# A first norm whose weights go on at the eviction, and norms and attention blocks moved into neighbouring stages of a two-layer trunk

## The chip, the cores and the metric

The kernel runs on one core of a Trainium2 chip. Its time is the device time of one execution, in microseconds (us); lower is better. Three runs of the kernel before gave 3104.6, 3106.2 and 3106.36 us, median 3106.2. Five engines work side by side, each through its own list of instructions: TensorE (PE in the profile, its weight loads PEld), VectorE (DVE), ScalarE (ACT), GpSimd (POOL) and SyncE (SP), which issues nearly all the DMAs.

## The reference

512 tokens of width 1024 pass two layers, in fp32. Layer 0 mixes by a convolution module and a gated linear attention; layer 1 by a forgetting attention (FoX, 16 heads of 64, causal, in query blocks of 128). Each layer ends with a PEER block: every token picks 128 of 16384 experts by product keys. Every mixing and every PEER block starts with an RMS norm, so there are four:

```
def rms_norm(x, g):
    y = x * rsqrt(mean(x * x, axis=-1, keepdims=True) + EPS)
    return y * g

h = rms_norm(x, ev_norm_mix);  x = x + even_mix(h, ...)      # norm 0, layer 0
h = rms_norm(x, ffn_norm[0]);  x = x + peer_ffn(h, ...)      # norm 1
h = rms_norm(x, od_norm_mix);  x = x + fox_mix(h, ...)       # norm 2, layer 1
h = rms_norm(x, ffn_norm[1]);  x = x + peer_ffn(h, ...)      # norm 3

# fox_mix, per head and query block i: softmax(q k^T * scale + c_q - c_k, causal) v, then o @ w_out
# peer_ffn: act = gelu(h @ u^T); out = (gate * act) @ v
```

## The kernel before

**Products.** fp32 operands are split in two parts, high and low (`split`, L51 and L52: ACT rounds the high part, DVE or POOL subtracts it to give the low one), and every product is three matmuls: high by high, low by high, high by low (`mm3`, L78, L79, L80). A weight tile is 128x1024: a DMA into `raw` (4 buffers), `whi` on ACT, `wlo` on DVE or POOL (3 buffers each).

**Tokens** lie in four blocks of 128 (`xb[0]` to `xb[3]`; block 0 stays in SBUF, the others are kept in DRAM during PEER). A norm (`rms_h`, `rms_body`) goes block by block. `scale(b)`: ACT squares the block and sums it (`sq`, L105), DVE makes the mean (`ss`, L106), POOL the power -0.5 (`rs`, L107), DVE multiplies the block by it and by the gains (`xs`, L108; the gains, `grow`, are one row broadcast to 128 partitions, a DMA of 512 KB, L86). `flip(b)`: PE transposes the block in eight 128x128 pieces, four into one PSUM bank (L115); ACT writes the high part `hhi` from the bank (L117), DVE the low part `hlo` (L118). The projections that follow contract over `hhi` and `hlo`.

**PSUM** has eight banks here: a pool `a` of six (scores, transposes and the accumulators of the projections) and a pool `b` of two.

**Stages.** Norm 0 and the layer-0 projections; the output projection of layer 0 (`out_proj`, two halves of the columns, c = 0 and 1, each four accumulators and weights in four slices; its additions to x are L200); norm 1; PEER of layer 0 (`peer`, `peer_body`): query projections (`q`, L928) interleaved with u tiles (`u_step`, accumulators `pu` over the 384 tokens of blocks 1 to 3, evicted by ACT through a gelu, L854), gathers of expert rows by DMA and, last, the sweeps over v tiles (`v_sweep`, L1033) into accumulators whose sums are added to x (L1062). Then norm 2, FoX, its output projection, norm 3 and the second PEER in the same way. In FoX one `unit()` is a score block of a head and a query block: scores (L640, L641) into one bank, row maximum on DVE (L643), exp on ACT (L646), reciprocal and scaling on DVE (L647, L648), transposes (L659) into another bank, a copy out (`PT`, L662 on ACT for four blocks, L664 on DVE for fewer), and the product with v (`po`, L672). Units are spread between the matmuls of the head projections; the last `8 + AHEAD + 1` come after the last projection and before `out_proj`.

**Order.** The program is written in Python and a scheduler orders each engine's instructions by simulated times; each engine then runs its list in that order, waiting at an instruction for what it reads. DMAs of one queue share semaphores in turn, so the ninth DMA issued waits for the first to land.

Of the kernel before, what the change touches and what calls it, by code (L numbers as in the profile page):

```python
# [45 lines left out]
class Trunk:  # L46
# [8 lines left out]
    def weight(self, src, shape=None, eng=None, after=None):  # L55

        nc = self.nc
        raw = self.ws.tile([P, D], F32, tag="raw", name="raw", bufs=4)
        self.last_raw = nc.sync.dma_start(raw, src)
        hi = self.ws.tile([P, D], F32R, tag="whi", name="whi", bufs=3)  # L60
        lo = self.ws.tile([P, D], F32R, tag="wlo", name="wlo", bufs=3)
# [26 lines left out]
    def rms_h(self, i, hT, h0=None, order=range(NB), after=None):  # L88


        with self.tc.tile_pool(name=f"rms{i}", bufs=1, reuse_waits="tile") as rp:
            self.rms_body(rp, i, hT, h0, order, after)
        if i + 1 < 4:
            self.load_gain(i + 1)

    def rms_body(self, rp, i, hT, h0, order, after):
        nc = self.nc
        xs = {}

        def scale(b):  # L100
            ss = self.np.tile([P, 1], F32, name="ss", bufs=NB)
            rs = self.np.tile([P, 1], F32, name="rs", bufs=NB)
            xs[b] = h0 if b == 0 and h0 is not None else rp.tile([P, D], F32, name="xs", bufs=2)
            sq = rp.tile([P, D], F32, name="sq")
            self.last_sq = nc.scalar.activation(sq, self.xb[b], AF.Square, accum_out=ss)  # L105
            nc.vector.tensor_scalar(ss, ss, 1.0 / D, EPS, op0=ALU.mult, op1=ALU.add)  # L106
            nc.gpsimd.tensor_tensor(rs, ss, self.mhalf, op=ALU.pow)  # L107
            nc.vector.scalar_tensor_tensor(xs[b], self.xb[b], rs, self.grow, op0=ALU.mult, op1=ALU.mult)  # L108

        def flip(b):  # L110
            for c in range(2):
                p = self.bank([P, 4, P])
                for k in range(4):
                    kk = (4 * c + k) * P
                    nc.tensor.transpose(p[:, k], xs[b][:, kk:kk + P], self.ident)  # L115
                hi, lo = [h[:, 4 * c:4 * c + 4, b * P:(b + 1) * P] for h in hT]
                nc.scalar.activation(hi, p, AF.Copy)  # L117
                nc.vector.tensor_tensor(lo, p, hi.bitcast(F32), op=ALU.subtract)  # L118

        scale(order[0])  # L120
        for n, b in enumerate(order):
            if n + 1 < NB:
                scale(order[n + 1])
            flip(b)
            if after:
                after(b)
# [27 lines left out]
    def nat_parts(self, srcs, hT, lead=0, order=range(4), done=None, between=None, eng=None):  # L154
        acc = [self.bank() for _ in range(NB)]

        def load(kps):
            return [(kp, *self.weight(srcs[kp], (2, 512), eng)) for kp in kps]

        def sweep(ws, blocks):  # L160
            for kp, wh, wl in ws:
                for a in range(2):
                    k = 2 * kp + a
                    for b in blocks:
                        s = slice(b * P, (b + 1) * P)
                        self.mm3(acc[b], hT[0][k][:, s], hT[1][k][:, s], wh[:, a], wl[:, a],
                                 kp == order[0] and a == 0, kp == order[-1] and a == 1)

        first = load(order[:lead])

        def rest():
            end = 1 if done else 4
            for kp in order[lead:end]:
                sweep(load([kp]), range(NB))
                if between:
                    between()
            if done:
                ws = load(order[end:])
                for b in BLOCKS:
                    sweep(ws, [b])  # L180
                    done(b, acc[b])
# [13 lines left out]
    def out_proj(self, w, yT, order=range(4)):  # L195
# [6 lines left out]
        for b, acc in enumerate(self.proj_nat(w[0], yT, order=order)):  # L202
            add(0, b, acc)
        self.proj_nat(w[1], yT, order=order, done=lambda b, acc: add(1, b, acc))
# [24 lines left out]
    def mix_even(self):  # L229
        nc, tc, A = self.nc, self.tc, self.A  # L230
        hT = self.new_hT()
        with tc.tile_pool(name="m0c", bufs=1) as sc:
            self.rms_h(0, hT)
            self.mix_even_body(hT, sc)

# [944 lines left out]
```

## Time and profile before

| | |
|---|---|
| median of three runs | 3106.2 us |
| the profiled execution: time, span, granted clock | 3103.41 us, 3101.6 us, 0.996 |
| PE busy | 3058.7 us, 99% of the span |
| DVE, ACT, POOL busy | 2401.2 (77%), 1384.7 (45%), 1096.6 us (35%) |
| HBM traffic | 253 GB/s over the span |

Span and busy times are of one execution. Part 4 of the page, the chain of work that ended last, lies for 92% on PE. Times in the rows are counted from the start of the span; `[idle before <-releaser]` at a row's end says how long the engine stood idle before it and what it waited for. PEclk is the granted clock of TensorE as a share of 2.4 GHz.

### The profile page before, as it was taken

Reading aid. Unit: us, or ns where it says so; the run is one execution under the profiler, and the core shown is the slowest. Engines: PE = TensorE matmul, PEld = TensorE weight load, DVE = VectorE, ACT = ScalarE, POOL = GpSimd, SP = SyncE. Lnnn points to the kernel's source line nnn. Section 1 sums busy time; section 2 is a strip of 40 time slices with the busy share of each in tenths; the row PEclk is TensorE's granted clock in tenths of the full one; section 3 lists DMA queues with packets and bytes.
Section 4 is the critical chain, followed back from the end, with each engine's and each line's share of the span. In section 5 each row is a group of like instructions: output and inputs, shape, how many; then the busy total and the mean of one; then the engine's idle time right before and its main releaser. Section 6 shows DMA issues by size and latency. Waiting matters only on the chain.

```text
span 3101.6 us, 45719 instructions
## 1 busy us (share of the span) xinstructions
PE 3058.7 (99%) x15932; PEld 2684.7 (87%) x15932; DVE 2401.2 (77%) x4936; ACT 1384.7 (45%) x2224; POOL 1096.6 (35%) x800
## 2 busy tenths in 40 slices
PE   8999999999999999999999999999999999999999
PEld 6668999999999888888776679999999998888887
DVE  6764998888886888888645638898888867888886
ACT  4444334666664333333344523336666653333332
POOL 1220122976674222222100000227866752222220
PEclk9999999999999999999999999999999999999999
DMA  4113444999999899999421124448999998999996
GB/s 158 55 35 116 137 144 159 353 363 336 343 320 329 298 356 363 366 363 370 172 82 42 42 78 142 137 142 311 380 336 345 336 326 278 356 369 357 376 363 219
DMA packets 334201, 787.15 MB, mean 254 GB/s; under 512 B 26745, under 2 KB 181770, under 8 KB 327826
## 3 DMA queue, kind: packets, MB, share of 16 engines
q1 hardware_dynamic: 260242, 515.76, 47.5%
q0 software_dynamic: 73728, 268.47, 24.5%
q8 instruction: 125, 2.05, 0.3%
q14 instruction: 106, 0.87, 0.1%
HBM read 687.59 MB, written 96.47 MB: 253 GB/s over the span
## 4 chain that ended last, share of the span: by engine, by line
PE 92%; DVE 3%; issue 2%; DMA 1%; POOL 1%; ACT 1%; DVEq 0%; POOLq 0%; ACTq 0%
PE acc L1033 32%; PE pu L79 11%; PE pu L80 11%; PE pu L78 11%; PE bank L78 6%; PE bank L80 5%; PE bank L79 5%; PE bank L912 5%; PE pc L285 1%; PE po L672 1%; PE bank L640 1%; PE bank L936 1%; DMA gr<-in_uN_dram,ids 1%; DVE wlo L52 1%; PE bank L659 1%
## 5 line engine op out<-in xcount | busy, mean ns | idle before, releaser
L51 ACT ACTIVATE whi<-raw 128x1024 fp32r<-128x1024 f32 x604 | 639.8, 1060 | 1500.6 <-issue 584.8
L52 DVE TENSOR_TENSOR wlo<-raw,whi 128x1024 fp32r<-128x1024 f32 x565 | 692.4, 1226 | 339.1 <-ACT whi L51 309.7
L78 PE MATMUL pu<-hhi,whi 128*128 128x384 f32 x2048 | 699.1, 341 | 1.2 <-ACT hhi L117 1.2
L80 PE MATMUL pu<-hhi,wlo 128*128 128x384 f32 x2048 | 688.2, 336 | 2.6 <-DVE wlo L52 2.6
L79 PE MATMUL pu<-hlo,whi 128*128 128x384 f32 x2048 | 686.8, 335 | 0.0
L873 POOL DMA_INDIRECT gr<-in_vF_dram,ids x256 | 277.0, 1082 | 720.8 <-DVE x L875 696.2
L1033 PE MATMUL acc<-wlo,wh 128*128 128x512 f32 x1536 | 439.2, 389 | 0.0
L1033 PE MATMUL acc<-whi,wh 128*128 128x512 f32 x1536 | 439.1, 389 | 0.0
L862 POOL DMA_INDIRECT gr<-in_uN_dram,ids x256 | 349.2, 1364 | 252.4 <-DVE dots L864 157.3
L1033 PE MATMUL acc<-whi,wl 128*128 128x512 f32 x1536 | 436.8, 389 | 0.0
L78 PEld LDWEIGHTS pu<-hhi,whi 128*128 128x128 f32 x2048 | 386.2, 189 | 3.0 <-ACT hhi L117 1.7
L80 PEld LDWEIGHTS pu<-hhi,wlo 128*128 128x128 f32 x2048 | 385.6, 188 | 3.4 <-DVE wlo L52 3.2
L79 PEld LDWEIGHTS pu<-hlo,whi 128*128 128x128 f32 x2048 | 386.2, 189 | 1.7 <-DVE hlo L118 0.3
L1033 PEld LDWEIGHTS acc<-whi,wl 128*128 128x128 f32 x1536 | 288.4, 188 | 59.9
L1033 PEld LDWEIGHTS acc<-wlo,wh 128*128 128x128 f32 x1536 | 288.4, 188 | 59.7
L1033 PEld LDWEIGHTS acc<-whi,wh 128*128 128x128 f32 x1536 | 288.4, 188 | 59.5
L875 DVE SCALAR_TENSOR_TENSOR x<-gr,dots,x 128x1024 f32<-128x1024 f32 x256 | 327.2, 1278 | 0.0
L864 DVE CUSTOM_DVE_ANT_0 gr<-gr,h 128x1024 f32<-128x1024 f32 x256 | 308.6, 1225 | 20.9 <-DMA gr<-in_uN_dram,ids 20.7
L902 POOL TENSOR_SCALAR a<-cst,sT 128x128 f32<-128x128 f32 x192 | 316.3, 1648 | 15.2 <-PE bank L912 5.6
L52 POOL TENSOR_TENSOR wlo<-raw,whi 128x1024 fp32r<-128x1024 f32 x39 | 98.1, 2515 | 396.1 <-ACT whi L51 388.1
L899 DVE TENSOR_TENSOR a<-cst,sT 128x512 f32<-128x512 f32 x192 | 133.4, 695 | 126.2 <-PE bank L912 114.8
L78 PE MATMUL bank<-hhi,whi 128*128 128x512 f32 x512 | 211.5, 414 | 3.5 <-DVE hlo L118 2.7
(244 smaller groups left out, 4095.7 us busy)
## 6 DMA issues: line engine op xcount, KB each, us to landing
raw<-in_uT_dram SPq DMA_DIRECT2D x256, 512.0 KB
raw<-in_vF_dram SPq DMA_DIRECT2D x256, 512.0 KB
G<-big SPq DMA_DIRECT2D x48, 1024.0 KB
gc<-G SPq DMA_DIRECT2D x32, 1536.0 KB
aside<-xact SPq DMA_DIRECT2D x208, 192.0 KB
at<-aside SPq DMA_DIRECT2D x104, 384.0 KB
raw<-in_w_in_dram SPq DMA_DIRECT2D x32, 512.0 KB
raw<-in_wq_dram SPq DMA_DIRECT2D x32, 512.0 KB
```

Of the source, the lines that this page charges most:

```text
L51: first = self.nc.scalar.activation(hi, raw, AF.Copy)
L52: self.last_lo = (eng or self.nc.vector).tensor_tensor(lo, raw, hi.bitcast(F32), op=ALU.subtract)
L78: mm(out, lh, rh, start=first, stop=False)
L79: mm(out, lh, rl, start=False, stop=False)
L80: return mm(out, ll, rh, start=False, stop=last)
L862: nc.gpsimd.indirect_dma_start(out=r, out_offset=None, in_=uN, in_offset=bass.IndirectOffsetOnAxis(ap=ids[:, s:s + 1], axis=0))
L864: return lambda: nc.vector.tensor_tensor_reduce(r, r, h0, 1.0, 0.0, ALU.mult, ALU.add, accum_out=dots[:, s:s + 1])
L873: nc.gpsimd.indirect_dma_start(out=r, out_offset=None, in_=vF, in_offset=bass.IndirectOffsetOnAxis(ap=ids[:, s:s + 1], axis=0))
L875: return lambda: nc.vector.scalar_tensor_tensor(self.x0, r, dots[:, s:s + 1], self.x0, op0=ALU.mult, op1=ALU.add)
L902: (nc.vector if t else nc.gpsimd).tensor_scalar(a1[:, t], self.iota, e1[:, t:t + 1], gate[:, t:t + 1], op0=ALU.is_equal, op1=ALU.mult)
L912: nc.tensor.matmul(p[:, t], a2[:, t], a1[:, t], start=True, stop=True)
L1033: nc.tensor.matmul(acc[b][c], wt[:, s], vt[:, c], start=(n == 0 and wt is wh and vt is vh), stop=(n == NE1 - 1 and wt is wl))
```

## The change

**First norm.** `first_norm` replaces `rms_h(0)`. The gains come as a column `gc` (128x8, 4 KB), x of blocks 1 to 3 is loaded right behind it, and four weight tiles before the other constants; the broadcast row is not loaded for this norm. The blocks are scaled by their token factor alone (`tensor_scalar`); the transposes go by the column tile k, four blocks into one bank, and the gain is applied at the eviction, where it is one number per partition: `scale=gc` on ACT, a `scalar_tensor_tensor` on DVE.

**The other norms** are built by `norm`, which gives out `scale` and `flip`, so that callers place them. Squares are written into the `xs` buffer instead of one of their own. Norm 2 is begun in the tail of the first PEER (`odd_begin`): block 0 is scaled and flipped between the last v sweeps, and the first two weight slices of the v projection get a pool of their own. Norm 3 is begun in the second half of the output projection (`ends`): blocks 1, 2, 3 are finished one after the other, each added, kept and scaled, and their flips stand between the matmuls of block 0; `chain` keeps this order on PE. The first `u_step` of each PEER stands before the flip of block 0.

**Attention.** The last twelve calls of `unit()` are made in the first half of the output projection, four behind each of three weight slices (`between`).

```
-    def rms_h(self, i, hT, h0=None, order=range(NB), after=None):
...
+    def norm(self, i, blocks=3):
...
+        def scale(b, dst=None):
...
+            xs[b] = rp.tile([P, D], F32, name="xs", bufs=blocks) if dst is None else dst
+            self.last_sq = nc.scalar.activation(xs[b], self.xb[b], AF.Square, accum_out=ss)
...
+        def flip(b, hT, other=False):
             for c in range(2):
-                p = self.bank([P, 4, P])
+                p = self.ps.tile([P, 4, P], F32, tag="b", name="fl", bufs=2) if other else self.bank([P, 4, P])
...
+    def chain(self):
+        last = []
+        def run(f, *args):
+            if last:
+                with self.tc.issue_after(last.pop().ins):
+                    last.append(f(*args))
...
+    def out_proj(self, w, yT, order=range(4), i=None, hT=None, between=None, middle=None):
...
+        def ends(sweeps, acc):
+            run = self.chain()
+            def finish(b):
+                add(1, b, acc[b])
+                if b:
+                    nc.sync.dma_start(self.kept[b - 1], self.xb[b])
+                    scale(b)
+            for b in DB:
+                for f in sweeps:
+                    run(f, b)
+                finish(b)
+            for n, f in enumerate(sweeps):
+                if n == 0:
+                    run(flip, 1, hT)
+                    run(flip, 2, hT)
+                if n == 2:
+                    run(flip, 3, hT)
+                run(f, 0)
+            finish(0)
...
+    def first_norm(self, gc, hT):
...
+                nc.vector.tensor_scalar(xs[b], self.xb[b], rs, None, op0=ALU.mult)
+            for k in range(KD):
+                p = self.bank([P, NB, P])
+                for b in range(NB):
+                    nc.tensor.transpose(p[:, b], xs[b][:, k * P:(k + 1) * P], self.ident)
+                p = p.rearrange("p b t -> p (b t)")
+                nc.scalar.activation(hT[0][:, k], p, AF.Copy, scale=gc[:, k:k + 1])
+                nc.vector.scalar_tensor_tensor(hT[1][:, k], p, gc[:, k:k + 1], hT[0][:, k].bitcast(F32),
+                                               op0=ALU.mult, op1=ALU.subtract)
...
-            for _ in range(8 + AHEAD + 1):
-                unit()
-            self.out_proj(A["w_out1"], self.rows(oT))
+            self.hT = self.new_hT()
+            self.out_proj(A["w_out1"], self.rows(oT), i=3, hT=self.hT, between=lambda: [unit() for _ in range(4)],
+                          middle=lambda: pool.__exit__(None, None, None))
...
+            if L == 0:
...
+                scale, flip, close = self.norm(1, 2)
+                scale(1)
+                for b in DB:
+                    scale((b + 1) % NB, None if b < NB - 1 else h0)
+                    flip(b, hT)
...
-        nu = 0
+        run(lambda: u_step(0)[1])
+        nu = 1
+        last()
...
         for b in range(nd):
-            v_sweep(tail, b)
+            run(v_sweep, tail, b)
...
+            if L == 0:
+                scale(DB[b])
+                if b == 1:
+                    run(put, 0, hN, True)
+        if L == 0:
+            for b in DB:
+                run(put, b, hN, True)
+                run(start, b - 1)
+            run(start, NB - 1)
```

`last` flips block 0 (`run(flip, 0, hT)`) and closes the norm's pools; `put` is the `flip` of norm 2 and `start(b)` the first eight products of block b in the v projection. The scheduler's order changes at the start, between layer 0 and its PEER, between that PEER and FoX, and from the last attention blocks into the second PEER; elsewhere the lists are the same but for the order of the very last v sweeps.

PE's list at the start, before: transposes (L115) come block by block, and the first products (L78 to L80) behind those of the fourth block; `wgh` is a small weight of the gate.

```order
L115 MATMUL bank<-cst,xs 128x128 [waits DVE_49]
L115 MATMUL bank<-cst,xs 128x128 x3
L115 MATMUL bank<-cst,xs 128x128 [waits PE_49]
L115 MATMUL bank<-cst,xs 128x128 x3
L78 MATMUL bank<-hhi,whi 128x512 [waits DVE_49,Activation_49]
L78 MATMUL bank<-hhi,whi 128x512 [waits DVE_49,PE_49]
L78 MATMUL bank<-hhi,wgh 16x512 [waits DVE_49]
L78 MATMUL bank<-hhi,whi 128x512 [waits DVE_49,PE_49,Activation_49]
L79 MATMUL bank<-hlo,whi 128x512 [waits DVE_49]
```

And of the change, the last transposes (L322) and the first products (L87 to L89):

```order
L322 MATMUL bank<-cst,xs 128x128 [waits DVE_49]
L322 MATMUL bank<-cst,xs 128x128 x5
L322 MATMUL bank<-cst,xs 128x128 [waits DVE_49]
L322 MATMUL bank<-cst,xs 128x128 x3
L322 MATMUL bank<-cst,xs 128x128 [waits DVE_49]
L322 MATMUL bank<-cst,xs 128x128 x3
L87 MATMUL bank<-hhi,whi 128x512 [waits DVE_49]
L88 MATMUL bank<-hlo,whi 128x512
L89 MATMUL bank<-hhi,wlo 128x512 [waits Pool_49]
```

The transposes of each block come in a run of six, and those of the last two column tiles behind them; the products of one weight tile then follow each other, one column tile after the other.

ACT's list from the end of the output projection of layer 1 into the second PEER, before: `sq` are the squares, `whi` the high parts of weights, `hhi` those of the norm, `q` the query projections, `xact` the gelus.

```order
L105 ACTIVATE sq,ss<-x_72 128x1024 [waits DVE_49,Activation_49]
L51 ACTIVATE whi<-raw 128x1024 [waits DMAHW1_49,PE_49]
L51 ACTIVATE whi<-raw 128x1024 [waits DMAHW2_49,PE_49]
L51 ACTIVATE whi<-raw 128x1024 [waits DMAHW3_49,PE_49]
L117 ACTIVATE hhi<-bank 128x4x128 [waits PE_49] x8
L51 ACTIVATE whi<-raw 128x1024 [waits DMAHW4_49,DVE_49,PE_49]
L51 ACTIVATE whi<-raw 128x1024 [waits DMAHW2_49,PE_49]
L928 ACTIVATE q<-bank 128x512 [waits PE_49]
L51 ACTIVATE whi<-raw 128x1024 [waits DMAHW3_49,PE_49]
L928 ACTIVATE q<-bank 128x512 [waits PE_49]
L854 ACT_TABLE_LOAD
L854 ACTIVATE xact<-pu 128x384 [waits PE_49]
```

And of the change, where L109 are the squares, L122 `hhi`, L1050 `q` and L972 the gelu:

```order
L122 ACTIVATE hhi<-bank 128x4x128 [waits PE_49]
L109 ACTIVATE xs,ss<-x 128x1024 [waits DVE_49]
L122 ACTIVATE hhi<-bank 128x4x128 [waits PE_49] x3
L53 ACTIVATE whi<-raw 128x1024 [waits DMAHW1_49,PE_49]
L122 ACTIVATE hhi<-bank 128x4x128 [waits PE_49] x2
L109 ACTIVATE h_16452,ss<-x_72 128x1024 [waits DMAHW3_49,DMAHW2_49,DMAHW4_49,DVE_49,Activation_49]
L53 ACTIVATE whi<-raw 128x1024 [waits DMAHW2_49,Activation_49]
L53 ACTIVATE whi<-raw 128x1024 [waits DMAHW3_49,Activation_49]
L53 ACTIVATE whi<-raw 128x1024 [waits DMAHW4_49,PE_49,Activation_49]
L972 ACT_TABLE_LOAD
L972 ACTIVATE xact<-pu 128x384 [waits PE_49]
L122 ACTIVATE hhi<-bank 128x4x128 [waits PE_49] x2
```

The eight `hhi` stood together ahead of all gelus; now six stand among the squares and weights, and the two of block 0 stand behind the table load and the first gelu. PE's list between the last attention blocks, before, has the scores (L640, L641), the transposes (L659) and `po` (L672) by themselves; these rows are from the end of that stretch, ahead of the output projection (L78 to L80 with `ohi`):

```order
L659 MATMUL bank<-cst,pr 128x128 [waits DVE_49,Activation_49]
L659 MATMUL bank<-cst,pr 128x128 x2
L640 MATMUL bank<-ka_14268,qa_14266 128x384 [waits PE_49]
L641 LDWEIGHTS idb
L641 MATMUL bank<-nmask,idb 128x128
L659 MATMUL bank<-cst,pr 128x128 [waits DVE_49,Activation_49]
L659 MATMUL bank<-cst,pr 128x128 x3
L640 MATMUL bank<-ka_14268,qa_14266 128x512 [waits PE_49]
L641 LDWEIGHTS idb
L641 MATMUL bank<-nmask,idb 128x128
L659 MATMUL bank<-cst,pr 128x128 [waits DVE_49,Activation_49]
L672 MATMUL po<-PT,v 64x512 [waits Activation_49]
```

Of the change, in the first half of the output projection (L87 to L89), scores are L747 and L748, transposes L766, `po` L779:

```order
L747 MATMUL bank<-ka_14264,qa_14262 128x384 [waits DVE_49]
L748 LDWEIGHTS idb
L748 MATMUL bank<-nmask,idb 128x128
L766 MATMUL bank<-cst,pr 128x128 [waits Activation_49]
L766 MATMUL bank<-cst,pr 128x128 x3
L747 MATMUL bank<-ka_14264,qa_14262 128x512 [waits Activation_49]
L748 LDWEIGHTS idb
L748 MATMUL bank<-nmask,idb 128x128
L779 MATMUL po<-PT,v 64x512
L779 MATMUL po<-PT,v 64x384
L779 MATMUL po<-PT,v 64x256
L779 MATMUL po<-PT,v 64x128
```

The last blocks now stand among the output projection's matmuls. There four of the six banks of pool `a` hold accumulators, so that scores and transposes take turns in the other two, and a row that waits for Activation or DVE next to another bank's use waits for the copy out of it.

## Rows read from the trace of the kernel before

**Rows 1.** the page: busy time of the engines, share of the span and instructions

```profile
PE 3058.7 (99%) x15932; PEld 2684.7 (87%) x15932; DVE 2401.2 (77%) x4936; ACT 1384.7 (45%) x2224; POOL 1096.6 (35%) x800
```

**Rows 2.** five stretches: length, busy time (instructions) by engine, granted clock, DMA share, GB/s

```profile
0.00:30.00 30.00, 14.86 (x50) 11.16 (x51) 15.30 (x22) 14.46 (x27) 5.89 (x10) 0.89 0.74 253
272.00:282.00 10.00, 5.42 (x31) 3.85 (x30) 9.68 (x13) 7.77 (x13) 0.55 (x1) 0.83 0.41 116
1525.00:1545.00 20.00, 16.66 (x86) 13.61 (x85) 13.62 (x18) 9.10 (x15) 10.61 (x6) 1.00 0.31 105
1764.00:1788.00 24.00, 22.97 (x114) 13.97 (x114) 17.81 (x52) 12.05 (x32) 0.00 (x0) 1.00 0.07 23
1836.00:1855.00 19.00, 12.97 (x59) 11.63 (x60) 13.81 (x20) 8.38 (x14) 3.21 (x4) 0.73 0.25 83
```

**Rows 3.** timeline of PE at the start: start us, us, what, idle before

```profile
20.44 0.50 PE L78 MATMUL bank<-hhi,whi 128*128 128x512 f32 x1 [0.88 <-ACT hhi L117]
...
24.62 0.80 PE L79 MATMUL bank<-hlo,whi 128*128 128x512 f32 x1 [0.87 <-DVE hlo L118]
...
29.06 0.54 PE L80 MATMUL bank<-hhi,wlo 128*128 128x512 f32 x1
...
29.67 0.40 PE L79 MATMUL bank<-hlo,whi 128*128 128x512 f32 x1
29.91 0.39 PE L80 MATMUL bank<-hhi,wlo 128*128 128x512 f32 x1
```

**Rows 4.** the same view of ACT, DVE and SP at the start

```profile
4.42 1.06 ACT L105 ACTIVATE sq<-x 128x1024 f32<-128x1024 f32 x1 [2.42 <-DMA x<-in_x_dram]
...
9.06 1.29 DVE L108 SCALAR_TENSOR_TENSOR xs<-x,rs,grow 128x1024 f32<-128x1024 f32 x1 [3.30 <-DMA grow<-in_gains_dram]
...
10.30 1.06 ACT L105 ACTIVATE sq<-x 128x1024 f32<-128x1024 f32 x1 [4.12 <-DMA x<-in_x_dram]
...
11.52 3.33 SPq L59 DMA_DIRECT2D raw<-in_w_in_dram  x4
```

**Rows 5.** timeline between layer 0 and its PEER, DVE and PE

```profile
276.21 3.49 DVE L52 TENSOR_TENSOR wlo<-raw,whi 128x1024 fp32r<-128x1024 f32 x3
...
280.45 1.30 PE L78 MATMUL bank<-hhi,whi 128*128 128x512 f32 x2 [1.53 <-DVE hlo L118]
```

**Rows 6.** timeline of PE in norm 2

```profile
1538.93 1.06 PE L115 MATMUL bank<-cst,xs 128*128 128x128 f32 x8 [1.83 <-DVE xs L108]
```

**Rows 7.** groups in the last attention blocks: busy us, mean ns, idle before

```profile
L643 DVE TENSOR_REDUCE nm<-bank 128x1 f32<-128x512 f32 x3 | 2.1, 685 | 0.6 <-PE bank L641 0.6
...
L646 ACT ACTIVATE pr<-bank,nm 128x512 f32<-128x512 f32 x3 | 2.1, 688 | 1.4 <-DVE nm L643 1.4
...
L648 DVE TENSOR_SCALAR pr<-pr,den 128x512 f32<-128x512 f32 x3 | 1.4, 483 | 0.1
...
L662 ACT ACTIVATE PT<-bank 128x512 f32<-128x512 f32 x4 | 2.4, 598 | 3.8 <-PE bank L659 3.8
```

**Rows 8.** timeline from the output projection of layer 1 into the second PEER

```profile
1835.19 0.40 PE L80 MATMUL bank<-whi,olo 128*128 128x512 f32 x1
...
1836.41 1.06 ACT L105 ACTIVATE sq<-x 128x1024 f32<-128x1024 f32 x1 [3.05 <-DVE ss L106]
...
1837.04 1.29 DVE L108 SCALAR_TENSOR_TENSOR xs<-x,rs,grow 128x1024 f32<-128x1024 f32 x1 [0.66 <-POOL rs L107]
...
1837.47 2.93 ACT L51 ACTIVATE whi<-raw 128x1024 fp32r<-128x1024 f32 x3
...
1838.39 4.66 PE L115 MATMUL bank<-cst,xs 128*128 128x128 f32 x24 [2.79 <-DVE ss L106]
...
1847.09 1.94 PE L115 MATMUL bank<-cst,h 128*128 128x128 f32 x8 [3.29 <-DVE hlo L118]
...
1854.57 0.33 PE L79 MATMUL pu<-hlo,whi 128*128 128x384 f32 x1
```

**Rows 9.** all groups of the span: the gelu's table loads

```profile
L854 ACT ACT_TABLE_LOAD x4 | 5.1, 1283 | 0.1
```

More of the change, by code (lines that the diff above doesn't have):

```diff
@@ L86, in load_gain @@
         self.nc.sync.dma_start(self.grow, self.A["gains"][i:i + 1].to_broadcast([P, D]))
[L88 to L96 removed]
+    def norm(self, i, blocks=3):
         nc = self.nc
+        pool = self.tc.tile_pool(name=f"rms{i}", bufs=1, side="right", reuse_waits="tile")
+        rp = pool.__enter__()
@@ L128, in new_hT @@
+    def chain(self):
[4 more added lines that the diff above has]
+                    last.append(f(*args))
+            else:
+                last.append(f(*args))
+            return last[0]
+        return run
     def new_hT(self):
@@ L152, in proj_nat, with nat_parts, load @@
         return rest()
[L154 to L158, printed above, removed]
+    def nat_parts(self, srcs, hT, lead=0, order=range(4), done=None, between=None, eng=None, pool=None):
+        acc = []
+        def load(kps, pool=None):
+            return [(kp, *self.weight(srcs[kp], (2, 512), None if pool else eng, pool=pool)) for kp in kps]
         def sweep(ws, blocks):
@@ L173, in rest @@
             for kp in order[lead:end]:
-                sweep(load([kp]), range(NB))
+                with self.tc.issue_after(self.last_put.ins) if pool else nullcontext():
+                    ws = load([kp])
+                sweep(ws, range(NB))
                 if between:
@@ L200, in add, with plain @@
             nc.vector.tensor_tensor(xa, xa, acc, op=ALU.add)
-        for b, acc in enumerate(self.proj_nat(w[0], yT, order=order)):
-            add(0, b, acc)
-        self.proj_nat(w[1], yT, order=order, done=lambda b, acc: add(1, b, acc))
+        def ends(sweeps, acc):
[17 more added lines that the diff above has]
+            finish(0)
+            self.run = run
+        def plain(sweeps, acc):
+            for b in BLOCKS:
+                for f in sweeps:
+                    f(b)
+                add(1, b, acc[b])
+        for b, acc in enumerate(self.proj_nat(w[0], yT, order=order, between=between)):
+            add(0, b, acc)
+        if middle:
+            middle()
+        if i is not None:
+            self.keep()
+            self.next_norm = scale, flip, _ = self.norm(i)
+        self.proj_nat(w[1], yT, order=order, done=plain if i is None else ends)
     def log_sigmoid(self, sp, z, shape, dst):
```

166 lines of the change are left out of this document (104 added, 62 removed).

## The prediction

> **What bounds the kernel now.** I read the page's busy times first: TensorE works 3058.7 us of a span of 3101.6 [rows 1], so 42.9 us are all that waits can give back, beside what a low clock costs. The waits of PE and the table of stretches come next, to see where those microseconds lie. The reader is to see a few short places: 15.1 us of the first 30 [rows 2], and then losses of a few microseconds where a norm stands between two stages. In the FoX norm PE lacks 3.34 us of 20; from 1836 to 1855 it lacks 6.0 of 19 and the granted clock is 0.73, from 272 to 282 it lacks 4.6 of 10 at 0.83 [rows 2]. A granted clock of 0.73 is a mix of the levels 2.4 and 1.2 GHz. Last come the timelines of these places, for the wait that ends last. Everything else in the program is dense PE work, whose order stays, so I price four norms and the end of attention, and nothing else.
>
> **Norm 0.** x of block 0 is there at 4.42, but DVE waits 3.30 us for the broadcast gains and scales at 9.06; block 1 lands at 10.30 [rows 4], and SyncE's queue, released by the landing of block 2, goes on at 11.52 [rows 4]: blocks land 1.2 to 1.3 us apart. PE's first product comes at 20.44, its dense run at 24.62, and the full clock is back at 29.06 [rows 3], 4.4 us after. From there products are 0.24 us apart (29.67, 29.91) [rows 3]; four were done ahead of 24.62, worth 0.9 us.
>
> After the change the broadcast of 512 KB is gone and x follows at once. Let X be the landing of block 3. The squares take 1.06 [rows 4], the mean and the power a little over 0.66 (DVE's wait for POOL between them and the scaling) [rows 8], the scaling at most 1.29 [rows 4]: about X+3.3. Six transposes, two conversions of weights of about 1 us ahead of the first eviction on ACT (three take 2.93 [rows 8]), one low part and the first low half on DVE follow: the first product near X+6.5, the run closed from X+7.3. I take the same 4.4 us to full clock: X+11.7. The ten or so products on the way are as many as now, the four early ones are not, so the gain is 29.06 - 0.9 - 11.7 - X = 16.4 - X. X is no row. The early end is three landings of 1.3 us behind 4.42, thus 8.3, gain 8.1; the late end is block 3 at the place of block 2, 11.5, gain 4.9. I take X = 10, between them, since the four weights issued right behind share the DMA engines: **+6.4**.
>
> **Norm 1.** Today's last wait is for `hlo` at 280.45 (1.53 us), because three low parts of weights (3.49 us from 276.21) stand ahead on DVE, which is busy 9.68 of 10 us [rows 2, 5]. The change pulls one low part forward and lets the first u product go ahead of block 0's flip. But the square of block 3 now writes into a buffer that the flip of block 1 must have left, and DVE's sum of work is the same. DVE remains the bound; I take -0.5, from +1.5 (that wait gone) to -1.8 (one more wait like that on `xs` in norm 2 [rows 6]).
>
> **Norm 2.** The 3.34 us [rows 2] are mostly waits for a scaled block, 1.83 the one at 1538.93 [rows 6]. Block 0's flip moves between v sweeps, which hides it. For the others, PE has 12 products (12 x 0.24 = 2.8) and 8 transposes (1.06 [rows 6]) per block, 3.9 us; the chain of a block is addition, square 1.06, the 0.66 for POOL, scaling 1.29, and the square stands behind the high halves of the block before on ACT (two of about 0.6, by the copy of the same size from PSUM [rows 7]): some 4.8. A deficit of 1 us, three times, is 3.0: **+0.3**, from +3.3 to -2.1 (three waits of 1.83).
>
> **Attention's end.** In the last dense blocks PE lacks 1.03 us of 24 [rows 2]. A block's chain is 0.69 maximum, 0.69 exp, 0.48 scaling, then transposes and a copy of 0.60 [rows 7]. Today six banks let the next scores be written while all that runs. In the first half of the output projection only two are left, so that a score row directly behind four transposes waits for their copy: 0.6 and the hand-over, about 0.8. In the new order I count four such places without products in between (0.8, 0.8, 0.65, 0.5) and some 0.2 elsewhere, 2.9 in all against 1.03: **-1.9**, from -0.5 to -4.
>
> **Norm 3.** Today the output projection ends at 1835.59 [rows 8]; PE stands 2.79 us for the first scaled block and 3.29 us for `hlo` [rows 8], and the first u step ends at 1854.74, 19.15 us on. Useful in that is 32 x 0.12 for transposes (8 in 1.06 with the tail of the last [rows 6]) = 3.8, 24 x 0.18 for u products (384 of 512 columns at 0.24) = 4.3, and 0.7 for two others: 10.4 us are lost, clock included.
>
> After, let T be the end of block 3's products; block 0's 24 products are still to do. Flips 1 and 2 fill T to T+1.9 (their blocks ended 5.6 and 11 us before), 12 products go to T+4.7. Block 3 is added at T+1.0, squared behind a high half on ACT by T+2.2, scaled by T+4.5: flip 3 is on time within 0.3. Its low half is late for the u step by 0.5. The u step ends near T+11.6; block 0's addition, square and scaling end near T+11.8: its flip loses about 0.5. Then the high halves of block 0 stand behind the first gelu on ACT: three weights (2.93 [rows 8]) to T+12.6, table load 1.28 [rows 9], gelu 0.5 (a copy of 512 columns takes 0.6 [rows 7], the gelu has 384), first half 0.6: T+15.0, while the first product that reads them could run at 13.1: 1.9. Sum 3.2, with small hand-overs 3.7. The clock: 0.83 over 10 us [rows 2] is 3.4 us at the lower level, half of it lost, 1.7; I count it half, 0.8. The gain is 10.4 - 3.7 - 0.8: **+5.9**, from +8.5 to +3.
>
> Two rules of the Trainium skill bear on this. ACT idles 3.05 us ahead of a square that waits for DVE, while three conversions of weights stand behind it and run only afterwards (1836.41, 1837.47) [rows 8]. "TensorE: Matmul & The Clock Gate" (Engine queue depths) has ACT and DVE as strict FIFOs; the trace agrees, and so the two high halves cannot pass the gelu. By the rule the norm brings 5.9, without it 7.8. The FoX norm runs at granted clock 1.00 with 3.3 us of waits in 20, the PEER norms at 0.73 and 0.83 [rows 2]. The same page (What's actually happening) says that the throttled clock is the default and activity releases it; if shorter waits mean no fall, the norm brings 6.7. I stay between, as rows 5 show a wait of only 1.53 in a stretch at 0.83.
>
> **Sum.** 6.4 - 0.5 + 0.3 - 1.9 + 5.9 = 10.2 us off the profiled execution's 3103.4. That lies 2.8 under the median of the runs shown; taken from the median, 3106.2 - 10.2 = **3096**. Kept blocks' DMAs move earlier beside projections; the DMA share around the norms is at most 0.41 [rows 2], so they cost nothing, and without that cover block 0 alone would see them. The gains for norm 1 are loaded later, well ahead of their use.
>
> **The rivals.**
> - *Earlier loads and hidden waits.* X at 8.3 (+1.7), norm 3 at 8.5 (+2.6), norm 2 with block 0 and one more wait hidden (+1.5), attention at -0.5 (+1.4): 7 more, 3089. For it: DMA moves only 0.74 of its time at the start [rows 2]. Against: it needs most terms at their end.
> - *The loads don't come earlier.* If the four weights take turns with x in the DMA engines, block 3 lands near 12.8 as now and norm 0 brings 3.6: 3099. For it: blocks land together today, 1.2 us apart, long after they were issued.
> - *Given back.* Attention loses 4 instead of 1.9, the wait behind the gelu lets the clock fall (1.7 + 2), norm 2 loses 2 instead of winning 0.3: about 7 back, 3103, no difference that counts.
> - *Two banks set attention's pace*, and the kernel is slower. Were every one of the last twelve blocks held in lockstep, each would wait its chain of 0.69 + 0.69 + 0.48 + 0.60 = 2.5 less the 0.6 of transposes: 1.9, or 22.8 in all, and the time 3096 + 20.9 = 3117. It decides above 1.0 us per block (12.1 for twelve), where the whole gain is used up. For it: today's idle is small only with six banks. Against: output-projection products of 0.24 stand between most of them.
>
> **Chances.** The forecast, with its own range 3092 to 3100, has 0.52; earlier loads 0.16; no earlier loads 0.10, half of it just faster, half not; given back 0.16; two banks 0.06. A difference under 0.2% (6.2 us) is about what a measurement of this kernel cannot tell from none: faster means under 3100.0, slower over 3112.4. Faster 0.52 + 0.16 + 0.05 = 0.73, same 0.16 + 0.05 = 0.21, slower 0.06. The range that holds 8 in 10 leaves out the last rival and the outer parts of the first and third: 3086 to 3104.
>
> **What will show it.** PE's dense run should start near 17 and be at full clock near 21.7; DVE's first scaling should follow its square and no DMA. From the end of the output projection to the end of the first u step PE should lack about 4 us, with one wait near 2 us for `hhi` behind a gelu. Idle in the last attention blocks should be near 3 us, on copies from PSUM. Wrong would be: block 3 landing behind 12, a granted clock under 0.9 after norm 3, or more than 5 us of PE idle in the first half of the output projection.

## The result, and the profile after

The changed kernel takes **3129.5 us** (median of 4 runs, 3126.7 to 3131.3) against 3106.0 for the kernel before: ratio 1.0073, interval 1.0060 to 1.0086. Forecast were 3096 and a range of 3086 to 3104. It is 23.5 us slower. The profiled execution took 3129.1 us; its span is 3127.3, 25.7 over that of before.

The busy row of the page answers to [rows 1]:

```profile
PE 3090.1 (99%) x15932; PEld 2682.5 (86%) x15932; DVE 2403.1 (77%) x4938; ACT 1385.3 (44%) x2222; POOL 1102.7 (35%) x800
```

TensorE executes as many instructions as before and is *busy* 31.4 us longer; its idle time fell from 42.9 to 37.2 us. A loss that sits in busy time stands in no list of waits. I therefore laid the two traces beside each other product by product, the i-th matmul of a stage in one against the i-th in the other, and looked where the distance between their starts changes. It shrinks at the norms, as forecast, and grows steadily through the v sweeps of both PEERs, where no wait is. The table of stretches in the middle of the two sweeps (length, PE's busy time and instructions, granted clock, DMA share, GB/s), first of before:

```profile
1200.00:1300.00 100.00, 100.00 (x443) 1.00 1.02 364
2800.00:2900.00 100.00, 100.00 (x443) 1.00 1.02 365
```

and of after:

```profile
1200.00:1300.00 100.00, 100.00 (x431) 1.00 1.00 353
2800.00:2900.00 100.00, 100.00 (x430) 1.00 1.00 352
```

PE is never idle and at full clock in both, and gets through 430.5 products instead of 443. The two sweeps have 2 x 2304 products: 4608 x (100/430.5 - 100/443) = **30.2 us**, more than the whole loss. The timeline of PE shows the step between products, first before:

```profile
1199.95 0.62 PE L1033 MATMUL acc<-wlo,wh 128*128 128x512 f32 x2
1200.40 0.61 PE L1033 MATMUL acc<-whi,wl 128*128 128x512 f32 x2
...
1201.76 0.61 PE L1033 MATMUL acc<-whi,wl 128*128 128x512 f32 x2
```

then after, the same products in the same order:

```profile
1199.87 0.63 PE L1156 MATMUL acc<-wlo,wh 128*128 128x512 f32 x2
1200.34 0.63 PE L1156 MATMUL acc<-whi,wl 128*128 128x512 f32 x2
...
1201.74 0.63 PE L1156 MATMUL acc<-whi,wl 128*128 128x512 f32 x2
```

Eight products take 1.81 us before and 1.87 after. Over all steps (from the start of one product to the start of the next) that are not broken by a gap the mean is 0.2267 and 0.2333 us.

The stretches that answer to [rows 2] (start, norms 1 and 2, the end of attention with the output projection's first half, norm 3):

```profile
0.00:30.00 30.00, 19.34 (x78) 15.14 (x79) 14.52 (x23) 16.07 (x26) 6.20 (x12) 0.94 0.67 236
265.00:275.00 10.00, 6.03 (x35) 4.75 (x33) 8.05 (x11) 7.67 (x14) 2.01 (x2) 0.78 0.41 117
1535.00:1555.00 20.00, 17.49 (x91) 13.80 (x90) 14.38 (x22) 8.38 (x16) 2.23 (x4) 1.00 0.21 76
1770.00:1827.00 57.00, 54.20 (x238) 36.03 (x237) 27.57 (x67) 19.54 (x46) 0.00 (x0) 1.00 0.15 47
1855.00:1875.00 20.00, 17.83 (x92) 15.66 (x92) 9.99 (x12) 9.77 (x13) 0.55 (x1) 1.00 0.49 165
```

These are the places that I had priced, and there the change wins time: the start lacks 10.7 us of 30 instead of 15.1, and norm 3 lacks 2.2 of 20 at clock 1.00 instead of 6.0 of 19 at 0.73. How well each term was priced is taken up further down.

### The profile page after: what moved, and what is told of

Read it like the earlier page. It is cut to its first block, busy times and chain, and to the rows that moved or that the text cites. A ratio compares the mean times of both kernels' runs of the same rounds, so it can differ in the third digit from the quotient of the medians.

```text
span 3127.3 us, 45688 instructions
## 1 busy us (share of the span) xinstructions
PE 3090.1 (99%) x15932; PEld 2682.5 (86%) x15932; DVE 2403.1 (77%) x4938; ACT 1385.3 (44%) x2222; POOL 1102.7 (35%) x800
## 4 chain that ended last, share of the span: by engine, by line
PE 91%; DMA 3%; DVE 3%; issue 1%; ACT 1%; POOL 1%; SPq 0%; DVEq 0%; POOLq 0%; ACTq 0%
PE acc L1156 34%; PE pu L87 10%; PE pu L88 10%; PE pu L89 10%; PE bank L87 5%; PE bank L88 5%; PE bank L89 5%; PE bank L1030 4%; DMA gr<-in_uN_dram,ids 3%; PE pc L376 1%; PE po L779 1%; PE bank L747 1%; PE bank L1058 1%; DVE wlo L54 1%; DVE gr L982 1%
## 5 line engine op out<-in xcount | busy, mean ns | idle before, releaser
L87 PE MATMUL pu<-hhi,whi 128*128 128x384 f32 x2048 | 699.7, 342 | 0.9 <-ACT hhi L122 0.9
L89 PE MATMUL pu<-hhi,wlo 128*128 128x384 f32 x2048 | 688.1, 336 | 2.2 <-DVE wlo L54 2.2
L1156 PE MATMUL acc<-whi,wh 128*128 128x512 f32 x1536 | 450.5, 396 | 0.0
L1156 PE MATMUL acc<-wlo,wh 128*128 128x512 f32 x1536 | 449.8, 395 | 0.0
L1156 PE MATMUL acc<-whi,wl 128*128 128x512 f32 x1536 | 448.2, 395 | 0.0
L87 PEld LDWEIGHTS pu<-hhi,whi 128*128 128x128 f32 x2048 | 385.6, 188 | 2.6 <-ACT hhi L122 1.3
L89 PEld LDWEIGHTS pu<-hhi,wlo 128*128 128x128 f32 x2048 | 384.8, 188 | 3.0 <-DVE wlo L54 2.8
L1020 POOL TENSOR_SCALAR a<-cst,sT 128x128 f32<-128x128 f32 x192 | 326.6, 1701 | 14.4 <-PE bank L1030 8.6
L87 PE MATMUL bank<-hhi,whi 128*128 128x512 f32 x512 | 211.0, 413 | 1.5 <-ACT hhi L122 1.5
```

The costliest lines, as they stand in the source:

```text
L87: mm(out, lh, rh, start=first, stop=False)
L89: return mm(out, ll, rh, start=False, stop=last)
L1020: (nc.vector if t else nc.gpsimd).tensor_scalar(a1[:, t], self.iota, e1[:, t:t + 1], gate[:, t:t + 1], op0=ALU.is_equal, op1=ALU.mult)
L1156: mm = nc.tensor.matmul(acc[b][c], wt[:, s], vt[:, c], start=(n == 0 and wt is wh and vt is vh), stop=(n == NE1 - 1 and wt is wl))
```

## The experiments

The change adds a tile of 32 bytes per partition, `gc0`, ahead of nearly everything else in SBUF, and moves `wh` and `wl` into a pool of their own. Both shift addresses, which the built programs list. In a v product `wh` or `wl` is the fixed operand and `whi` or `wlo` (a v tile) streams past it. Before, `wh` begins at byte 188448 of a partition and `whi` at 42784; after, at 163904 and 42784 (their other buffers follow at multiples of 256 bytes). My theory after the result: these addresses set the step of 0.227 or 0.233 us. The rival: the order or the company of the sweeps (the new pool, the gathers).

**Gain column of 128 bytes** (the changed kernel).

```diff
-        gc = self.np.tile([P, KD], F32, name="gc0")
+        gc = self.np.tile([P, 32], F32, name="gc0")[:, :KD]
```

> The changed kernel, its gain column allocated with 128 bytes per partition instead of 32; nothing else. Every tile allocated behind it moves by 96 bytes. Theory (addresses): a 512-column matmul takes 0.2333 us instead of 0.2267 where its stationary and moving tiles start at different places modulo 128 bytes; the 32 bytes of the gain column moved wh and wl from 32 to 64 while the v tiles stayed at 32. With 128 bytes they agree again: 2 x 2304 v products x 0.0067 = 30.7 us back, about 3098.5 us, spacing 0.2267. If the gates stage was slowed by the same shift, 4 more: 3094. Rival (pools): the v sweeps are slower because wh and wl come from a pool of their own, by its waits and not its place: unchanged, 3129, spacing 0.2333.

Measured: 3123.9 us, ratio 1.0063 (1.0046 to 1.0080); the step is 0.2324. The theory in this form, remainders by 128, failed.

**The same shift in the kernel before**: 32 unused bytes ahead of the pools of the stages.

```diff
+            pad = self.np.tile([P, 8], F32, name="pad", bufs=1)
+            nc.gpsimd.memset(pad, 0.0)
             self.x0 = cp.tile([P, D], F32, name="x0")
```

> The kernel before, with an unused tile of 32 bytes per partition ahead of the gains' row, so that all later tiles move by 32 bytes, in the same order of instructions. Theory (addresses): the v sweeps go to 0.2333, the time to 3106 + 30.7 = 3137 us, up to 3141 if the gates stage suffers too. Rival (pools): 3106, spacing 0.2267.

Measured: 3138.4 us, ratio 1.0107 (1.0090 to 1.0124), step 0.2333. Nothing of the change is in this kernel, and it loses all that the changed one loses in the sweeps. Its stretch:

```profile
1200.00:1300.00 100.00, 100.00 (x430) 1.00 1.00 355
```

**All tiles shifted**: the same 32 bytes, but ahead of the weights too, so that both operands move together.

```diff
             stf = cp.tile([P, 2, TOPK], F32, name="stf")
+            pad = cp.tile([P, 8], F32, name="pad")
+            nc.gpsimd.memset(pad, 0.0)
```

> The kernel before, with an unused tile of 32 bytes per partition ahead of the weight tiles, so that weights, hhi, hlo, wh and wl all move by 32 bytes, to 64 modulo 128, and still agree. If only the difference of the two addresses counts: 3106 us within 3, spacing 0.2267 in the v sweeps and the projections. If the place itself counts (32 modulo 128 is the good one): all the dense products go to 0.2333, at least 30.7 us more for the v sweeps and some 20 us for projections and u products, 3150 or more. Rival (pools): 3106.

Measured: 3106.1 us, ratio 1.0003 (0.9993 to 1.0012), step 0.2267. Not the place counts, but the relation of the two operands' places.

**`wh` and `wl` alone, by 96 bytes** (the changed kernel).

```diff
                 wb, vb = wpool.__enter__(), vpool.__enter__()
+                pad = wb.tile([P, 24], F32, name="pad", bufs=1)
+                nc.gpsimd.memset(pad, 0.0)
```

> The changed kernel, with an unused tile of 96 bytes per partition at the start of the pool of wh and wl, which puts these (and the gate tiles behind them) back to 32 modulo 128; everything ahead stays where the change put it. Theory (addresses): v sweeps at 0.2267, 3098.5 us; the gates stage keeps its 2 us per PEER. If it comes out like the run with 128 bytes for the gain column, the gates stage has nothing to do with addresses. Rival (pools): 3129.

Measured: 3123.0 us, ratio 1.0061 (1.0044 to 1.0078), step 0.2324: the same address of `wh` as with the 128 bytes, 164000, and the same answer. Both addresses leave the same remainder by 128 and are 128 apart by 256. What is left by these four runs is a remainder by 256 or more.

**Gain column of 256 bytes.**

```diff
-        gc = self.np.tile([P, KD], F32, name="gc0")
+        gc = self.np.tile([P, 64], F32, name="gc0")[:, :KD]
```

> The changed kernel, with one edit: the tile of the first norm's gain column is 256 bytes wide instead of 32, so that the tiles behind it are 224 bytes further up, and wh and wl of the v sweeps have the same remainder by 256 as the weights that stream past them. Theory (what counts is that remainder): a 512-column v product takes 0.227 us as before, not 0.233, 2304 of them twice win 30 us, and the time is 3096 to 3100, faster than before by the gains of the norms. Rival (the v sweeps pay for their own pool, or for what stands beside them, not for the remainder): 0.2325 to 0.2335 us and 3122 to 3130, as in the runs with 128 bytes.

Measured: **3095.6 us**, ratio 0.9964 (0.9950 to 0.9978), step 0.2267:

```profile
1200.00:1300.00 100.00, 100.00 (x443) 1.00 1.03 365
```

One number in one line turns 23.5 us slower into 11.7 us faster, and the time is the one forecast for the change without that cost.

**`wh` and `wl` alone, by 224 bytes**, with 32 behind them, so that the gathered gates and activations, which lie further up, move by 256 in all and keep the remainder that they have in the changed kernel.

```diff
-                wb, vb = wpool.__enter__(), vpool.__enter__()
+                wb = wpool.__enter__()
+                pad = wb.tile([P, 56], F32, name="pad", bufs=1)
...
+                vb = vpool.__enter__()
...
+        pad = wb.tile([P, 8], F32, name="pae", bufs=1)
         vpool.__exit__(None, None, None)
```

> The changed kernel with 224 bytes ahead of wh and 32 behind wl in their pool, so that wh and wl alone get the remainder of whi and wlo by 256, while the other tiles of the v sweeps (gathered gates, activations) keep theirs. Theory (fixed against streaming operand alone): 0.227 us per v product, 443 products in 100 us, 3097 to 3101. Rival (the tiles that DMAs and the other engines write beside them count): 430 to 432 products, 3122 to 3130.

Measured: 3098.9 us, ratio 0.9976 (0.9967 to 0.9985), step 0.2267 and 443 products in 100 us. The two operands decide, not their neighbours.

**`wl` off by 32 bytes, `wh` not**: the pad of 224 stays, and the pad of 32 now lies between them.

```diff
             wh = wb.tile([P, TD], F32R, name="wh")
...
+                pad = wb.tile([P, 8], F32, name="pae", bufs=1)
...
             wl = wb.tile([P, TD], F32R, name="wl")
```

> As the run with wh and wl aligned, but wl alone is 32 bytes off. Theory (each product pays for its own pair): the products with wl, one in three, take 0.233 and the others 0.227, 10 us over the run with both aligned. Rival (what counts is the stream beside the load of the next weights): also two in six, 10 us, but the slow ones are the last product on wh and the first on wl. A third (one tile off slows the whole sweep): 30 us.

Measured: 3115.8 us, ratio 1.0028 (1.0017 to 1.0039), 16.9 over the run before it: none of the three. The stretch and the timeline:

```profile
1200.00:1300.00 100.00, 100.00 (x434) 1.00 1.01 358
```

```profile
1199.65 0.62 PE L1164 MATMUL acc<-whi,wl 128*128 128x512 f32 x2
1200.11 0.62 PE L1164 MATMUL acc<-whi,wh 128*128 128x512 f32 x2
1200.58 0.63 PE L1164 MATMUL acc<-wlo,wh 128*128 128x512 f32 x2
1201.05 0.62 PE L1164 MATMUL acc<-whi,wl 128*128 128x512 f32 x2
1201.51 0.63 PE L1164 MATMUL acc<-whi,wh 128*128 128x512 f32 x2
```

Here the products alternate by two, and eight take 1.86 us, those on the aligned `wh` no less than those on `wl`. For some v tiles the scheduler put six products of a kind in a row:

```profile
1286.32 1.53 PE L1164 MATMUL acc<-whi,wh 128*128 128x512 f32 x6
1287.68 1.53 PE L1164 MATMUL acc<-wlo,wh 128*128 128x512 f32 x6
1289.05 1.56 PE L1164 MATMUL acc<-whi,wl 128*128 128x512 f32 x6
1290.45 1.53 PE L1164 MATMUL acc<-whi,wh 128*128 128x512 f32 x6
```

There, in the trace's nanoseconds, the mean step is 227.4 and 228.1 on `wh` and 232.4 on `wl`. On `wh` nearly all of the excess lies at the borders: the last product ahead of the six on `wl` takes 235.0, the first behind them 231.0, and the others 226.7 to 226.9. So a pair that is off also slows its neighbours. The slow product ahead is what one would see if the load of the next fixed operand beside the stream were slowed; the slow one behind does not follow from that, and the reason stays open.

**All other pairs aligned too**: `ohi` and `olo`, and the lead weights of FoX, by unused tiles of 192 bytes beside the 256 of the gain column.

```diff
+            pad = sp.tile([P, 48], F32, name="pad")
...
             oT = sp.tile([P, KD, T], F32R, name="ohi"), sp.tile([P, KD, T], F32R, name="olo")
...
+        pad = lead.tile([P, 48], F32, name="pad", bufs=1)
```

> As the run with 256 bytes, and two unused tiles of 192 bytes bring ohi and olo (the output projection of layer 1) and vhi and vlo (the first weights of the FoX v projection) to the same remainder by 256 as their partners. Theory: 192 and 48 products go from 0.233 to 0.227 us, which is 1.5 us less than the run with 256 bytes. Rival: only the v sweeps are sensitive, those products stay at 0.233, and the two runs agree within 0.5 us.

Measured: 3096.0 us, ratio 0.9963 (0.9951 to 0.9976). The steps of these 240 products fell to 0.2286, 1.2 us in sum; a time that is known to about 4 us can't show it. The trace bears most of the theory out, the time neither way.

What all runs together say of the step, by the distance of the two addresses (fixed less streaming, remainder by 256):

| fixed and streaming operand, where | distance by 256 | us per product |
|---|---|---|
| `wh`, `whi`: before; both shifted; 256 bytes; 224 bytes | 0 | 0.2267 |
| `ohi`, `whi`: all aligned; with attention first | 0 | 0.2285; 0.2272 |
| `wh`, `whi`: after; before with 32 bytes | 32 | 0.2333 |
| `ohi`, `whi`: before | 64 | 0.2333 |
| `hhi`, `vhi`: after | 64 | 0.2332 |
| `ohi`, `whi`: after | 96 | 0.2342 |
| `wh`, `whi`: 128 bytes; 96 bytes | 128 | 0.2324 |
| `ohi`, `whi`: 128 bytes | 192 | 0.2296 |

The last row stands apart: at 192 the products of the output projection are only 0.001 us slower than the same ones at 0 with the same neighbours (0.2285). Not every distance costs the same, and 64 and 192 are not alike.

Next come the terms of my sum.

**Norm 0 alone**, put into the kernel before (with the gain column of 256 bytes).

> The kernel before with the first norm of the changed kernel alone (gain column of 256 bytes, x and four weights loaded first, the gain applied at the eviction, the step constants built on POOL ahead of the first PEER norm); everything else stays, remainders too. My prediction's step for norm 0: 6.4 us, 3099.5. Rival (what is won at the start is given back: the loads of the gains for norm 1 and of the constants come later, or the clock falls elsewhere): 3102 or more.

Measured: 3099.7 us, ratio 0.9977 (0.9968 to 0.9986), 7.1 us faster by the ratio: the size of this step was right.

**Attention's last steps ahead of the output projection**, with 256 bytes.

```diff
+            for _ in range(8 + AHEAD + 1):
+                unit()
             self.out_proj(A["w_out1"], self.rows(oT), i=3, hT=self.hT,
-                          between=lambda: [unit() for _ in range(4)],
```

> As the run with 256 bytes, but the last thirteen steps of attention run ahead of the output projection, as in the kernel before, with six banks. My prediction's step (two banks cost attention 2.9 us of waits against 1.0): 1.9 us faster than the run with 256 bytes. Rival (the waits between the products cost nothing more than the ones they replace, or the chain of the last block then waits at the start of the projection): the same within 0.7 us or slower.

Measured: 3092.5 us, ratio 0.9951 (0.9937 to 0.9965). It is 3.2 us less than with the steps inside, but the two intervals overlap. The waits say more. With the steps inside (us in total, times, longest), from 1765 to 1815:

```profile
PE bank L747 <- ACT PT L769: 1.4, 2, 0.7
PE bank L747 <- DVE PT L771: 0.6, 1, 0.6
PE bank L87 <- ACT ohi L783: 0.4, 1, 0.4
PE bank L87 <- DVE PT L771: 0.2, 1, 0.2
PE bank L766 <- DVE PT L771: 0.2, 1, 0.2
```

and ahead, from 1760 to 1812:

```profile
PE bank L766 <- DVE den L754: 0.6, 1, 0.6
PE bank L747 <- issue: 0.4, 1, 0.4
```

2.8 against 1.0 is the 1.8 that I had put at 1.9. But the waits are not the whole cost: by the distance between the same matmuls, the steps inside cost 4.4 us (under norm 3, further down).

**Both edits together.**

> The two edits that helped, together: every fixed tile at the remainder of its partner, and attention's last steps ahead of the output projection. If they add up (3.2 for the steps, 1.2 for 240 products that go from 0.2334 to 0.2285): 3090 to 3092, ratio to the kernel before near 0.995. Rival (the steps ahead and the projection's faster products have one answer, since the projection then waits for its last block): as with the steps alone, 3092.5.

Measured: 3093.3 us, ratio 0.9960 (0.9946 to 0.9973). Whether they add up is below what these times can tell.

**The first gelu late.** The activation is issued behind the flip of block 0.

```diff
-            self.last_act = nc.scalar.activation(a, p, AF.Gelu)
...
+            def act():
+                self.last_act = nc.scalar.activation(a, p, AF.Gelu)
...
+            if e == 0:
+                self.act0 = act
...
         last()
+        self.act0()
```

> As the run with both edits, and the first gelu of each PEER stage is issued behind the high halves of the norm's last block on ACT, instead of ahead of them. My prediction's step (these halves cannot pass the gelu and its table load, which costs the product that reads them 1.9 us; the trace of the changed kernel shows a wait of 1.47 us on hhi): 1.4 to 1.9 us faster than the run without. Rival (the wait turns into one on hlo from DVE, which comes next behind it): within 0.5 us.

Measured: 3091.1 us, ratio 0.9950 (0.9936 to 0.9964). It looks like the 1.9 expected, and isn't: ACT's timeline has the old order, the scheduler having moved the gelu forward again.

```profile
1837.93 1.28 ACT L981 ACT_TABLE_LOAD   x1
1839.23 0.49 ACT L981 ACTIVATE xact<-pu 128x384 f32<-128x384 f32 x1
1839.61 1.08 ACT L122 ACTIVATE hhi<-bank 128x512 fp32r<-128x512 f32 x2
```

So the 2 us between these two kernels is not this edit's. Bound to the last high half, the gelu did go behind:

```diff
-        self.act0()
+        with tc.issue_after(self.last_put.ins):
+            self.act0()
```

> As the run with both edits (all tiles aligned, attention's last steps first), and in the second PEER stage the last two high halves of the norm now do stand ahead of the gelu's table load on ACT; in the run called gelu late the order of ACT had stayed as it was. My prediction's step: the wait of 1.5 us on hhi at the first product that reads block 0 goes, 1.4 to 1.9 us. Rival (the low halves on DVE, which start behind the high ones and behind three low parts of weights, are late next): a wait on hlo of about 1 us stands in its place, and less than 0.7 us is won. A gain of that size is in the trace's wait; the times of single builds differ by about 2 us without it.

Measured: 3092.2 us, ratio 0.9956 (0.9942 to 0.9969). PE's waits there:

```profile
PE pu L89 <- DVE wlo L54: 1.3, 1, 1.3
PE bank L120 <- DVE h L112: 0.4, 1, 0.4
PE pu L88 <- DVE hlo L123: 0.3, 1, 0.3
```

The 1.5 us on `hhi` are gone, and 1.26 for the low part of a weight stand in their place, the last of three that DVE makes in 3.49 us. It is the rival, with another tile than I had named.

## Why the prediction was wrong

**The step that failed** is the sentence "Everything else in the program is dense PE work, whose order stays, so I price four norms and the end of attention, and nothing else." The order did stay, and the dense work was slowed all the same, by an address. The experiments show it from both sides: 32 bytes in the kernel before cost what the change loses in the v sweeps, and 224 bytes more in the kernel after give it back. The diff had the tile and the pool, and the trace of before had a hint: the same 512-column product took 0.2333 in the output projection and 0.2267 in the v sweeps. I used one figure, 0.24, for all of them. No rival had it either: "two banks set attention's pace" is slower at 3117 by waits, and waits there are 2.8 us.

**The terms**, by the distance between the same products in the two traces:

| stage | predicted | in the trace |
|---|---|---|
| norm 0 | +6.4 | +6.2 |
| norm 1 | -0.5 | +0.3 |
| norm 2 | +0.3 | +0.6 |
| attention's end and norm 3 | +4.0 | +3.6 |
| FoX, ahead of attention | 0 | -1.6 |
| gates in the u stages of both PEERs | 0 | -4.2 |
| v sweeps of both PEERs | 0 | -30.6 |
| sum | +10.2 | -25.7 |

*Norm 0.* The rows that answer to [rows 3, 4], of ACT and then of PE:

```profile
9.63 1.06 ACT L315 ACTIVATE xs<-x 128x1024 f32<-128x1024 f32 x1
```

```profile
7.19 1.54 PE L322 MATMUL bank<-cst,xs 128*128 128x128 f32 x6 [7.19 <-DVE xs L318]
...
16.69 1.31 PE L322 MATMUL bank<-cst,xs 128*128 128x128 f32 x8 [2.42 <-DVE hlo L325]
18.01 0.75 PE L87 MATMUL bank<-hhi,whi 128*128 128x512 f32 x1
...
21.53 0.39 PE L89 MATMUL bank<-hhi,wlo 128*128 128x512 f32 x1
21.76 0.39 PE L87 MATMUL bank<-hhi,whi 128*128 128x512 f32 x1
```

Block 3 had landed by 9.6 (I took X = 10), and full clock comes at 21.5 (I said 21.7). Between the two the estimate missed twice: the first product came at 18.0 and not near 16.5, after a wait of 2.42 us for `hlo`, and full clock 3.5 us behind it, where I had taken 4.4 us from a closed run at 17.3. The two errors cancel, so that 6.2 for 6.4 is in part luck.

*Norms 1 and 2.* In norm 1 the last wait, 1.53 for `hlo` [rows 5], is now 0.90 for `hhi`; that DVE would go on setting the end was wrong, by 0.8 us:

```profile
269.98 1.35 PE L120 MATMUL bank<-cst,xs 128*128 128x128 f32 x8 [3.04 <-DVE ss L110]
272.24 0.69 PE L87 MATMUL pu<-hhi,whi 128*128 128x384 f32 x1 [0.90 <-ACT hhi L122]
```

In norm 2 two waits of 1.20 and 1.21 are left, where I had three of 1.0 and [rows 6] had 1.83.

*Norm 3.* The wait that I had named is there, at 1.47 for 1.9; ACT's rows, then PE's:

```profile
1857.64 2.98 ACT L53 ACTIVATE whi<-raw 128x1024 fp32r<-128x1024 f32 x3
1860.63 1.28 ACT L972 ACT_TABLE_LOAD   x1
1861.93 0.49 ACT L972 ACTIVATE xact<-pu 128x384 f32<-128x384 f32 x1
1862.32 1.08 ACT L122 ACTIVATE hhi<-bank 128x512 fp32r<-128x512 f32 x2
```

```profile
1860.08 1.06 PE L120 MATMUL bank<-cst,h 128*128 128x128 f32 x8 [0.43 <-DVE h L112]
...
1862.96 0.74 PE L87 MATMUL bank<-hhi,whi 128*128 128x512 f32 x2 [1.47 <-ACT hhi L122]
```

With the halves ahead of the gelu, 0.25 us of waits was won and not the 1.9 that lie between my 5.9 and 7.8. The granted clock stayed at 1.00 through these waits. The Trainium skill ("TensorE: Matmul & The Clock Gate", What's actually happening) has the throttled clock as the default and activity as what releases it; the trace agrees in so far as waits this short brought no fall here. But the same wait of 1.4 us in FoX (on `pr`) went with a granted clock of 0.74 in the 5 us around it after, and 1.00 before.

The +3.6 for attention's end and norm 3 hides two errors. The same 705 matmuls of TensorE, from the last attention blocks into the second PEER, in the kernel before, with 256 bytes, and with 256 bytes and attention's steps ahead (length, PE's busy time and instructions, granted clock, DMA share, GB/s):

```profile
1750.00:1905.00 155.00, 147.53 (x705) 0.97 0.26 86
1746.44:1897.69 151.25, 145.44 (x705) 1.00 0.27 90
1744.77:1891.63 146.86, 143.64 (x705) 1.00 0.27 91
```

Norm 3 by itself wins 155.0 - 146.9 = 8.1 us, where I had 5.9: its waits are 2.2 us in all (1.47, 0.43 and 0.3) for my 3.7, and the fall of the clock for which I had counted 0.8 did not come. Attention's steps inside the output projection cost 151.3 - 146.9 = 4.4 us, where I had 1.9 and at worst 4: 2.6 of it is idle time and 1.8 longer steps of a busy TensorE, for which my sum had no term. That the two together came near +4.0 is luck.

**What stays open.** That fall is the -1.6 of FoX. The wait stands in all fifteen profiles; the granted clock of the 45 us around it is 0.96 in eight of them and 1.00 in seven. The kernel before is among the seven, and the run with all tiles shifted, which is the kernel before at other addresses, among the eight; so the fall comes without the change too. The gates (PE waits there for POOL's `a`, L1020) lost 2.2 and 2.0 us against before. In the other builds' single profiles the two losses lie between -1.4 and 4.3, and the run with 256 bytes, with 2.8 and 2.3, has the forecast time. About 0.6 us of this loss is no wait but a steady drift. The changed kernel and the runs with 32, 128, 96 and 224 bytes and with `wl` off have it, the others don't; so it goes with the addresses, though which products pay is not shown. I can't tell from one profile per build what of the rest is the change's. Without the v sweeps these two profiles are 4.9 us apart and not 10.2; that the total comes out as forecast rests on the medians, 11.7 us with 256 bytes.

## What to carry to other kernels

Where TensorE is busy all the time, compare the rate of a dense stretch (instructions in 100 us) before any list of waits. A change that adds or moves a tile changes the addresses of all tiles behind it in SBUF; for split fp32 products of 512 columns keep the fixed and the streaming operand at the same remainder by 256 bytes, and round small tiles up to 256 bytes so that later ones keep theirs. Take differences of 2 us between builds of such a kernel from the traces, not from their times, and there from the distance between the same matmuls: the list of waits showed 1.8 of the 4.4 us that attention's steps cost.

The version that beats both is the changed kernel with the 256-byte gain column: 3095.6 us. Those with attention's last steps ahead of the output projection as well have 3091.1 to 3093.3, in four builds.

## What the hardware showed that I had not expected

- The step between 512-column products is 0.2267 us in the v sweeps where the two operands' addresses agree by 256, 0.2324 at 128 apart, and 0.2332 to 0.2342 at 32, 64 and 96: 2.5 to 3.3 per cent, in the v sweeps with the clock at 1.00 and PE busy throughout. At 192 it is 0.2296, beside 0.2285 for the same products at 0. The Trainium skill ("SBUF — State Buffer", Operand start alignment) asks only that an operand start at a multiple of its element size, and says that its runs timed nothing; all addresses here fulfil that, and the time differs.
- A product whose own operands agree is slowed too when its neighbours' don't: about 0.232 where they alternate by two, 0.2350 and 0.2310 right ahead of and behind a row of six.
- This one is of the scheduler and not of the chip: an instruction issued later in the program can be scheduled back to where it was, as the first gelu was. The order in the trace has to be read before a time is believed.
